# A gated linear unit over 8192 rows: four-row groups packed in place in three slots, instead of two input slots and two output slots

## The chip, the cores and the metric

The kernel runs on one core of a Trainium2 chip. The metric is the device time in microseconds of one execution of the whole program; lower is better. The profile is taken from an execution of its own, and its span (from the first to the last instruction that it records) is a little shorter than the device time.

## What is computed

The input `x` has 8192 x 8192 float32 values. Each row is cut into two halves, `a` (the first 4096 columns) and `b` (the last 4096), and the output has 8192 x 4096 values:

```python
def reference(x):
    a, b = np.split(x, 2, axis=-1)
    return a * (1 / (1 + np.exp(-b)))
```

That is one sigmoid and one multiplication for each output value. 268.4 MB are read and 134.2 MB written, with no value used twice.

## The kernel before

Two consecutive rows go to each of the 128 partitions, so a tile is 256 rows, 8 MB of input and 4 MB of output, and there are 32 tiles. Two slots hold input tiles (64 KB per partition each), two more hold output tiles (32 KB per partition each): 192 KB per partition in all.

```python
    R = 2
    SLOTS = 2
    n_tiles = n_rows // (P * R)
    x_t = x.rearrange("(n p r) m -> n p (r m)", p=P, r=R)
    out_t = out.rearrange("(n p r) m -> n p (r m)", p=P, r=R)
    xs = [pool.tile([P, R * n_cols], fp32, name=f"x_sb{k}") for k in range(SLOTS)]
    os = [pool.tile([P, R * half], fp32, name=f"o_sb{k}") for k in range(SLOTS)]
    ...
    for i in range(n_tiles):
        ...
        load = nc.sync.dma_start(out=xs[i % SLOTS], in_=x_t[i])
        ...
        if 0 < i < n_tiles - 1:
            parts = [(slice(0, R), slice(0, half))]
        else:
            w = half // 2
            parts = [
                (slice(r, r + 1), slice(c * w, (c + 1) * w)) for r in range(R) for c in range(2)
            ]
        ...
        for k, (r, c) in enumerate(parts):
            b = rows[:, r, 1, c]
            sig = nc.scalar.activation(out=b, in_=b, func=SIG)
            mul = nc.vector.tensor_mul(out=packed[:, r, c], in0=rows[:, r, 0, c], in1=b)
            ...
            if i == n_tiles - 1 and k > 0:
                store(chunks[k - 1])
        store(chunks[-1] if i == n_tiles - 1 else slice(0, R * half))
```

Loads are issued by SyncE (SP), stores by ScalarE (ACT), each on its own DMA queue. ACT computes the sigmoid of `b` in place, VectorE (DVE) multiplies into the output slot. A tile is one sigmoid and one multiplication of 8192 elements per partition (both rows); the first and the last tile are done in four pieces of 2048, and the last tile's output is stored piece by piece. A load into a slot waits for the multiplication that last read the slot; a multiplication or a sigmoid waits for the store that last read the output slot. Most of the other code in the loop (`implied`, `add_manual_dep`) names waits that follow from these and are dropped. `_launch_early` moves the first load ahead of the start-up barrier, and `_close_on_sync` shortens the end of the program; both stay as they are.

Of the kernel before, what the change touches and what calls it, by code (L numbers as in the profile page):

```python
# [1 line left out]

# [4 lines left out]


def _tiles(ctx, tc, x, out):

    nc = tc.nc
    P = nc.NUM_PARTITIONS  # L20
    DEP = mybir.DependencyInfo(mybir.DependencyClass.Sync, mybir.DependencyReason.DATA)
    fp32 = mybir.dt.float32
    SIG = mybir.ActivationFunctionType.Sigmoid

    n_rows, n_cols = x.shape
    half = n_cols // 2
    R = 2
    SLOTS = 2
    n_tiles = n_rows // (P * R)
    x_t = x.rearrange("(n p r) m -> n p (r m)", p=P, r=R)  # L30
    out_t = out.rearrange("(n p r) m -> n p (r m)", p=P, r=R)

    pool = ctx.enter_context(tc.tile_pool(name="io", bufs=1))
    xs = [pool.tile([P, R * n_cols], fp32, name=f"x_sb{k}") for k in range(SLOTS)]
    os = [pool.tile([P, R * half], fp32, name=f"o_sb{k}") for k in range(SLOTS)]

    def implied(later, *earlier):
        for e in earlier:
            tc.declare_no_dep(later.ins, e.ins, reason="follows from the waits that are kept")

    gone = [{k: [] for k in ("loads", "sigs", "muls", "stores")} for _ in range(SLOTS)]
    last_stores = [[] for _ in range(SLOTS)]
    for i in range(n_tiles):
        old = gone[i % SLOTS]
        freed = last_stores[i % SLOTS]
        now = {k: [] for k in old}
        rows = xs[i % SLOTS].rearrange("p (r h m) -> p r h m", r=R, h=2)
        packed = os[i % SLOTS].rearrange("p (r m) -> p r m", r=R)

        load = nc.sync.dma_start(out=xs[i % SLOTS], in_=x_t[i])  # L50
        implied(load, *old["loads"], *old["sigs"])
        now["loads"].append(load)

        if 0 < i < n_tiles - 1:
            parts = [(slice(0, R), slice(0, half))]
        else:
            w = half // 2
            parts = [
                (slice(r, r + 1), slice(c * w, (c + 1) * w)) for r in range(R) for c in range(2)
            ]  # L60
        def store(cols):
            ins = nc.scalar.dma_start(out=out_t[i, :, cols], in_=os[i % SLOTS][:, cols])  # L62
            now["stores"].append(ins)

        chunks = []
        for k, (r, c) in enumerate(parts):
            b = rows[:, r, 1, c]
            sig = nc.scalar.activation(out=b, in_=b, func=SIG)  # L68
            mul = nc.vector.tensor_mul(out=packed[:, r, c], in0=rows[:, r, 0, c], in1=b)  # L69
            implied(sig, *old["sigs"], *old["muls"], *old["loads"])  # L70
            implied(mul, *old["muls"], *old["loads"], *now["loads"])
            by_sigmoid = i % 2 == 1 and len(parts) == 1
            implied(mul, *(s for s in old["stores"] if by_sigmoid or s not in freed))
            if by_sigmoid:
                for s in freed:
                    tc.add_manual_dep(sig.ins, s.ins.name, DEP, reason="frees the output slot")
            tc.keep_in_program_order(sig)
            now["sigs"].append(sig)
            now["muls"].append(mul)
            chunks.append(slice(r.start * half + c.start, r.start * half + c.stop))  # L80
            if i == n_tiles - 1 and k > 0:
                store(chunks[k - 1])
        store(chunks[-1] if i == n_tiles - 1 else slice(0, R * half))
        for s in now["stores"]:
            implied(s, *old["loads"], *old["sigs"], *old["muls"], *now["loads"], *now["sigs"])
        for k in old:
            old[k] += now[k]
        last_stores[i % SLOTS] = now["stores"]


def _launch_early(nc):

    SP = mybir.EngineType.SP
    entry, body = (b.instructions for b in nc.main_func.blocks[:2])
    load = next(i for i in body if i.engine == SP and i.opcode == "DMACopy")
    assert not load.sync_info.on_wait
    body.remove(load)
    where = next(k for k, i in enumerate(entry) if i.engine == SP and i.opcode == "Drain")  # L100
    entry.insert(where, load)


def _close_on_sync(nc):

    SP, POOL = mybir.EngineType.SP, mybir.EngineType.Pool  # L110
    ACT = mybir.EngineType.Activation
    block = nc.main_func.blocks[2].instructions
    waits = block[0]
    assert waits.engine == SP and waits.opcode == "Drain" and len(waits.sync_info.on_wait) > 1
    pool = [i for i in block if i.engine == POOL]
    drain1, gather1, release1, reset, clear, drain2, gather2, release2 = pool
    assert reset.is_reset_sema and clear.opcode == "ISA"
    others = [i for i in block[1:] if i.engine != POOL]
    arrive = [i for i in others[: len(others) // 2] if i.opcode == "Drain"]
    assert len(arrive) == 4  # L120
    body = nc.main_func.blocks[1].instructions
    last = [i for i in body if i.engine == ACT and i.opcode == "DMACopy"][-1].sync_info.on_update[0].id
    final = [w for w in waits.sync_info.on_wait if w.id == last]
    assert len(final) == 1

    def event(engine, wait, update=()):
        return mybir.InstEventSemaphore(
            name=nc.get_next_instruction_name(),
            engine=engine,
            debug=waits.debug,  # L130
            sync_info=mybir.SyncInfo(on_wait=[wait], on_update=list(update)),
        )

    n = len(block)
    for lo, hi in ((reset.reset_range_start, last), (last + 1, reset.reset_range_stop)):
        if lo < hi:
            nc.gpsimd.sem_clear(range(lo, hi))
    clears = block[n:]
    assert clears and all(i.opcode == "ISA" for i in clears)
    back = mybir.SyncUpdate(  # L140
        sync_type="semaphore",
        id=last,
        ant_name=final[0].ant_name,
        update_mode="sem-sub-imm",
        update_value=final[0].wait_value,
        update_reg=None,
    )
    block[:] = [
        *arrive,
        drain1,  # L150
        gather1,
        *(event(POOL, w) for w in waits.sync_info.on_wait if w.id != last),
        reset,
        *clears,
        drain2,
        event(SP, final[0], [back]),
    ]


@with_exitstack  # L160
def kernel(
    ctx: ExitStack,
    tc: tile.TileContext,
    x: bass.AP,
    out: bass.AP,
):
    nc = tc.nc
    with ExitStack() as pools:
        _tiles(pools, tc, x, out)
    tc.close()  # L170
    tc.compile()
    _launch_early(nc)
    _close_on_sync(nc)


# [1 line left out]
_INS = ['x']  # L177
_OUTS = [((8192, 4096), 'float32')]


# [23 lines left out]
```

## Time and profile before

| What | Value |
|---|---|
| Device time, median of 3 (lowest, highest) | 933.31 us (933.03, 933.4) |
| Span of the profiled execution | 931.7 us |
| DVE busy | 278.7 us, 38 multiplications |
| ACT busy | 227.1 us, 38 sigmoids and a table load |
| Sigmoid and multiplication of 8192 elements | 7031 ns and 8692 ns |
| Sigmoid and multiplication of 2048 elements | 1903 ns and 2288 ns |
| SP's queue waiting for a multiplication | 859.9 us in total, 30 times |

How to read it: "busy" is the time in which an engine executes; the issuing of a DMA isn't counted. DMA queue q1 is SP's and carries the loads, q10 is ACT's and carries the stores. The share of a queue is the time that its packets took, as a share of 16 DMA engines over the span. "To landing" is the time from the issue of a DMA to its completion. A line number such as L69 is a line of the kernel.

### The profile page before, as it was taken

The numbers are of one execution on the slowest core, as the hardware profiler recorded it, in microseconds if no ns is written. First come the engines' busy times: TensorE is split into PE (matmuls) and PEld (weight loads), VectorE is DVE, ScalarE is ACT, GpSimd is POOL, SyncE is SP. The second block draws the span as 40 slices with busy tenths as digits, with TensorE's granted clock in tenths as the row PEclk, the third lists the DMA queues.
The fourth block names the chain that finished last, engine by engine and source line by source line (L and its number), as shares of the span: only waits on it lengthen the run. The fifth ranks groups of instructions, "written<-read, shape, count | busy, mean of one in ns | idle before, by whom it ended". The sixth has DMA issues, their size and how long they took to land.

```text
span 931.7 us, 247 instructions
## 1 busy us (share of the span) xinstructions
DVE 278.7 (30%) x38; ACT 227.1 (24%) x39; POOL 0.2 (0%) x4
## 2 busy tenths in 40 slices
DVE  0333213333133331233312333123331233312333
ACT  1323330233311333113331133311333113332033
POOL 0000000000000000000000000000000000000000
DMA  9999999999999999999999999999999999999999
GB/s 405 428 450 428 422 456 405 450 428 428 450 418 438 428 436 442 428 428 450 447 408 428 442 459 428 413 460 411 450 428 425 453 408 447 428 428 450 425 430 405
DMA packets 9649, 402.67 MB, mean 432 GB/s; under 512 B 1072, under 2 KB 1072, under 8 KB 1072
## 3 DMA queue, kind: packets, MB, share of 16 engines
q1 hardware_dynamic: 4608, 268.44, 66.6%
q10 hardware_dynamic: 5040, 134.22, 33.4%
q14 instruction: 1, 0.01, 0.0%
HBM read 268.44 MB, written 134.22 MB: 432 GB/s over the span
## 4 chain that ended last, share of the span: by engine, by line
DMA 73%; DVE 15%; ACT 12%; issue 0%; ACTq 0%
DMA x_sb<-in_x_dram 73%; DVE o_sb L69 15%; ACT x_sb L68 12%; ACTq L62 0%; ACTq L68 0%
## 5 line engine op out<-in xcount | busy, mean ns | idle before, releaser
L69 DVE TENSOR_TENSOR o_sb<-x_sb 128x8192 f32<-128x8192 f32 (+1 forms) x38 | 278.7, 7344 | 647.1 <-ACT x_sb L68 647.1
L68 ACT ACTIVATE x_sb<-x_sb 128x8192 f32<-128x8192 f32 (+1 forms) x38 | 225.8, 5952 | 695.6 <-DMA x_sb<-in_x_dram 694.4
L68 ACT ACT_TABLE_LOAD x1 | 1.3, 1283 | 0.8 <-PEq L188 0.8
L188 POOL MEMSET const-bfloat16-1.0<- 128x1 bf16 x1 | 0.1, 102 | 0.0
L188 POOL MEMSET const-uint8-127<- 128x1 uint8 x1 | 0.1, 102 | 0.0
L188 POOL MEMSET const-float32-0.0<- 128x1 f32 x1 | 0.1, 99 | 0.2 <-issue 0.2
L188 POOL MEMSET const-float32-1.0<- 128x1 f32 x1 | 0.1, 99 | 0.0
## 6 DMA issues: line engine op xcount, KB each, us to landing
out_dram<-o_sb ACTq DMA_DIRECT2D x31, 4096.0 KB, 34.7
out_dram<-o_sb ACTq DMA_DIRECT2D x4, 1024.0 KB, 5.6
x_sb<-in_x_dram SPq DMA_DIRECT2D x32, 42.2
```

The lines of the kernel that those rows point to most:

```text
L68: sig = nc.scalar.activation(out=b, in_=b, func=SIG)
L69: mul = nc.vector.tensor_mul(out=packed[:, r, c], in0=rows[:, r, 0, c], in1=b)
L188: nc = _bacc.Bacc("TRN2", target_bir_lowering=False, num_devices=1)
```

## The change

Rows are taken in groups of four per partition (512 rows, 16 groups). A group's input is loaded in two halves of two rows, 8 MB each. There are three slots of 64 KB per partition, 192 KB in all as before: two called `firsts`, used in turn for the first half of a group, and one called `second` for every second half. There are no output slots. The products are written in place: those of the first half over the beginning of the group's `firsts` slot, those of the second half over its end, so that after both halves the slot holds the four output rows, packed. One store of 8 MB then writes them, 64 KB from each partition, and for each partition both ends of the store are contiguous. The purpose is to have fewer and larger stores, and to use the memory of the output slots for a third load slot.

Every half is computed row by row: two sigmoids and two multiplications of 4096 elements, where before one of each covered both rows.

A load into `second` waits for the multiplications that read `second`. A load into a `firsts` slot waits for the store that reads the slot; both loads are issued by SP in the order second half, then the next-but-one first half.

In the last group, the first half is stored by itself (4 MB) and by SP, whose queue then holds the last load ahead of it; the second half is computed in four pieces of 2048 elements and stored by ACT piece by piece, 1 MB each.

The core of the diff (cut; the lines that only declared which waits follow from others are removed with the rest of the old loop):

```diff
-    SLOTS = 2
-    n_tiles = n_rows // (P * R)
-    x_t = x.rearrange("(n p r) m -> n p (r m)", p=P, r=R)
-    out_t = out.rearrange("(n p r) m -> n p (r m)", p=P, r=R)
+    n_groups = n_rows // (P * 2 * R)
+    x_t = x.rearrange("(n p h r) m -> n h p (r m)", p=P, h=2, r=R)
+    out_t = out.rearrange("(n p h r) m -> n p (h r m)", p=P, h=2, r=R)
...
-    xs = [pool.tile([P, R * n_cols], fp32, name=f"x_sb{k}") for k in range(SLOTS)]
-    os = [pool.tile([P, R * half], fp32, name=f"o_sb{k}") for k in range(SLOTS)]
+    firsts = [pool.tile([P, R * n_cols], fp32, name=f"first{k}") for k in range(2)]
+    second = pool.tile([P, R * n_cols], fp32, name="second")
...
+    def load(g, h):
+        nc.sync.dma_start(out=second if h else firsts[g % 2], in_=x_t[g, h])
+
+    def compute(g, h, pieces, each=None):
+        src = second if h else firsts[g % 2]
+        rows = src.rearrange("p (r k m) -> p r k m", r=R, k=2)
+        packed = firsts[g % 2].rearrange("p (h r m) -> p h r m", h=2, r=R)[:, h]
+        w = half // pieces
+        for r in range(R):
+            for c in range(pieces):
+                cols = slice(c * w, (c + 1) * w)
+                b = rows[:, r, 1, cols]
+                sig = nc.scalar.activation(out=b, in_=b, func=SIG)
+                tc.keep_in_program_order(sig)
+                nc.vector.tensor_mul(out=packed[:, r, cols], in0=rows[:, r, 0, cols], in1=b)
+                if each is not None:
+                    each((h * R + r) * half + c * w, w)
+
+    def store(engine, g, lo, n):
+        engine.dma_start(out=out_t[g, :, lo : lo + n], in_=firsts[g % 2][:, lo : lo + n])
+
+    load(0, 0)
+    load(0, 1)
+    load(1, 0)
+    for g in range(n_groups):
+        last = g == n_groups - 1
+        compute(g, 0, 1)
+        if last:
+            store(nc.sync, g, 0, R * half)
+            waiting = []
+
+            def each(lo, n):
+                if waiting:
+                    store(nc.scalar, g, *waiting.pop())
+                waiting.append((lo, n))
+
+            compute(g, 1, 2, each)
+            store(nc.scalar, g, *waiting.pop())
+        else:
+            compute(g, 1, 1)
+            store(nc.scalar, g, 0, 2 * R * half)
+            load(g + 1, 1)
+            if g + 2 < n_groups:
+                load(g + 2, 0)
```

More of the change, by code (lines that the diff above doesn't have):

```diff
@@ L20, in _tiles @@
     P = nc.NUM_PARTITIONS
-    DEP = mybir.DependencyInfo(mybir.DependencyClass.Sync, mybir.DependencyReason.DATA)
     fp32 = mybir.dt.float32
@@ L35, in _tiles @@
-    os = [pool.tile([P, R * half], fp32, name=f"o_sb{k}") for k in range(SLOTS)]
[L37 to L55, printed above, removed]
-        else:
[L57 to L88, printed above, removed]
```

## The prediction

> **What bounds the kernel now.** I read the page's DMA lines first, because the two compute engines are busy only 30% and 24% of the span, then the chain, then the times to landing, then the stretches.
>
> ```profile
> span 931.7 us, 247 instructions
> ...
> DMA  9999999999999999999999999999999999999999
> ...
> DMA packets 9649, 402.67 MB, mean 432 GB/s; under 512 B 1072, under 2 KB 1072, under 8 KB 1072
> ...
> q1 hardware_dynamic: 4608, 268.44, 66.6%
> q10 hardware_dynamic: 5040, 134.22, 33.4%
> ...
> DMA 73%; DVE 15%; ACT 12%; issue 0%; ACTq 0%
> ...
> out_dram<-o_sb ACTq DMA_DIRECT2D x31, 4096.0 KB, 34.7
> out_dram<-o_sb ACTq DMA_DIRECT2D x4, 1024.0 KB, 5.6
> x_sb<-in_x_dram SPq DMA_DIRECT2D x32, 42.2
> ```
>
> All 40 slices have full DMA engines, and the shares of the two queues (q1 is SP's loads, q10 ACT's stores) add up to 100%. The chain seems to say otherwise, with 27% on ACT and DVE. But that chain only follows one load to the next through a sigmoid and a multiply; while they run, the other slot's load and the stores keep the DMA engines fed. The stretches confirm it (columns: stretch, its length, three engines' busy time with instructions, clock, DMA share, GB/s):
>
> ```profile
> 0.00:22.00 22.00, 0.00 (x0) 1.33 (x2) 0.20 (x4) 1.00 1.02 429
> 22.00:42.00 20.00, 8.90 (x4) 7.26 (x4) 0.00 (x0) 1.00 0.95 393
> 42.00:100.00 58.00, 17.39 (x2) 14.06 (x2) 0.00 (x0) 1.00 1.00 434
> 100.00:900.00 800.00, 241.70 (x28) 196.87 (x28) 0.00 (x0) 1.00 1.00 434
> 900.00:932.00 32.00, 10.68 (x5) 7.54 (x4) 0.00 (x0) 1.00 0.95 410
> ```
>
> From 42 to 900 us the rate is 434 GB/s without a break. 402.67 MB at 434 GB/s take 927.8 us, so of the 931.7 us only about 4 lie in the start and the end. No reordering can win much more than that; a change can, however, open gaps.
>
> **Why there is no gap now** is in the landing times. A load is issued every 29 us (two tiles in the 58.0 us from one same-slot load to the next in the chain) and takes 42.2 us to land; a store is issued every 29 us and takes 34.7. Both take longer than the interval, so neither queue runs empty: when a new load is issued, the one ahead of it has 42.2 - 29.0 = 13.2 us left. Nothing that is late by less than 13 us shows.
>
> **What the Trainium skill says.** "DMA: Bandwidth & Descriptors", section "Where 436 GB/s comes from", puts the ceiling at 435.2 GB/s; the trace's 434 agrees, so the middle is at the wall. The same page, "Queues, rings and completion order", says that each DMA engine alternates between the queues that have work, packet by packet. The trace agrees: q1's time is 0.666 x 16 x 931.7 us over 4096 packets of 64 KB (4608 less 512 completion writes), 2.42 us each; q10's, less 512 packets of 8 KB at 0.31, is 1.21 us for each of 3968 packets of 32 KB. One for one, that shares the traffic 2:1, just what loads and stores need. "Issuing engines are not separate DMA queues" says that a second queue adds no bandwidth; the sum of 100% agrees. The same page, "Latency and other measured facts", reports that copies within HBM lose rate where the partitions' row pitch is a large power of two (207 GB/s at 512 KiB, 214 with a padded pitch). The new loads have a pitch of 128 KiB where they had 64; no run here shows its effect, and I allow it a small chance only.
>
> **The change part by part.**
>
> 1. *Bytes and packets.* The bytes stay. Stores become 64 KB packets: 15 x 128 of them replace 30 x 128 of 32 KB. By the times above, 3840 x 1.213 - 1920 x 2.418 = 15 us of engine time, over 16 engines about 1 us. The last group keeps 4 MB in one and 4 MB in four pieces. **-1 us.**
>
> 2. *Row by row.* Sigmoids of 8192 elements take 7031 ns and of 2048, 1903; multiplies 8692 and 2288. By straight line, 4096 elements cost an estimated 3.61 and 4.42 us. A half is ready 3.6 + 2 x 4.42 = 12.5 us after its sigmoid starts, instead of 15.7. It costs an issue more per half on engines that idle 70% of the time: nothing. With 0.41 us from landing to sigmoid (before: landing 914.30, sigmoid 914.71) and 0.1 for the issue, 13.0 us pass from the landing of a second half to the next issues.
>
> 3. *Start.* Three loads, 24 packets deep on each engine, are queued from about 1.9 us; they last until 60 us. The second half of group 0 lands at 40.6, so the first store leaves at 53.6. No gap; the first store comes later, which saves nothing as the wall is bytes.
>
> 4. *End.* The first half's store stands in SP's queue behind the last load: 4 MB, 9.7 us of work, while the last half is computed. Pieces come after 0.4 + 1.9 + 2.3 = 4.6 us and then every 2.3 us, four of them up to 11.5 us, each 2.4 us of traffic. Work at hand until the last piece is 9.7 + 3 x 2.4 = 17 us: no gap. Before, tile 30's store (issued 901.7) filled the same stretch as well. **0 us.**
>
> 5. *The cycle of one group*, the step on which the answer turns. A group moves 16 load packets and 8 store packets per engine, 24 x 2.418 = 58.0 us. Let both issues be at 0: the 8 MB store, and the load into `second`; the load of the next first half is still in flight with X packets. The store's packets now weigh as much as the load's. Its first one starts some 4 to 6 us late: for the only store of before that met an empty queue, issued at 32.8, this shows:
>
> ```profile
> q1 hardware_dynamic: 32, 2.10, 85.1%
> q10 hardware_dynamic: 16, 0.52, 18.1%
> ```
>
> Those are the DMA packets from 32.8 to 39.5 us: two load packets per engine, then the first store packet, which the same view up to 38.8 does not have yet. So 6 us from issue to first packet; and the two load packets fill 0.851 x 16 x 6.7 / 32 = 2.85 us each instead of 2.42, a stall of about 0.9 us in all. Then 8 rounds of store and load, 8 x 4.84 = 38.7 us. With a typical 5 us ahead of them the store lands at 43.7 (44.7 with the stall). **Only then** may the load of group g+2's first half go, since its slot is the store's source. Its data flow 2.0 to 2.6 us after the issue (the first load of before: 21.9 to landing less 8 x 2.418), thus at about F = 46. But when is the queue empty? The second half's load lands at L, and the next issues are at L + 13.0. Without a gap the period is 58.0, so L = 45.0. That is before F: slack has shrunk from 13.2 us to about -1. A later L lets less of the next load run, half is given back: L = (45.0 + F)/2 = 45.5, and the period grows by **0.5 us**. With the 0.9 us stall in every group, F = 47 and L = (45.0 + 0.9 + 47)/2 = 46.5: **1.4 us**. With a quick first packet (3.7 us) F = 44.8: **0**. Fourteen groups wait so: 0, 7 or 20 us.
>
> *Sum:* 933.3 - 1.0 + 14 x 0.5 = 939.3; I take 940.0.
>
> **The rivals.** (a) *All hidden:* the store starts sooner, or a load issued just in time slips behind the running one: 932 us. For it: the needed slack is a single microsecond and the numbers are single observations. (b) *A stall at each restart of the store queue:* 933.3 - 1.0 + 20 = 952 us. For it: the stall was there the one time that an empty store queue was refilled; against it: that was the queue's first use. (c) *The memory dislikes 128 KiB pitch:* 1% of the loads' 620 us (0.666 x 931.7) would be 6 us, beside the others; visible as longer load packets. (d) *A compute engine binds:* 66 multiplies cost about 62 x 4.42 + 4 x 2.29 = 283 us of DVE; it cannot. (e) *Faster by the shorter latency:* the latency was hidden already, and the wall leaves 4 us.
>
> **Range and chances.** (a) gets 30%, the middle case 40%, (b) and beyond 30%. Two per cent is 18.7 us: faster needs 914.6, under the 925.2 us that the bytes take at 435.2 GB/s, as good as excluded. Slower needs over 952.0, where (b) has its centre: 15%. Range 931.5 to 955.
>
> **What would show it.** DMA share under 1.00 in the middle stretch, some 0.99 for 940 (434 becomes about 430 GB/s); 8192 KB stores landing after about 44 us; loads of `second` landing 45 to 46 us after issue; SP's queue waiting mostly for the store. Sigmoids and multiplies of 4096 at 3.6 and 4.4 us. Step 5 is wrong if the stores land after under 42 us or over 47, or if the middle stretch stays at 434; then 932 would be the time. A load packet that lasts longer than 2.42 us would mean (c). If store packets were split to 32 KB, the store would get a third of the traffic and land after some 60 us, and the time would go far above the range.

## The result and the profile after

The changed kernel takes 968.02 us (median of 4 runs, 964.2 to 968.68) against 933.36 us: 1.036 times the time, with a 95% interval of 1.034 to 1.038. The prediction, 940 us with a range up to 955, was too low by 28 us.

The page of the changed kernel, the lines that answer to those shown of before:

```profile
span 967.3 us, 310 instructions
...
DMA packets 7490, 402.67 MB, mean 416 GB/s; under 512 B 832, under 2 KB 832, under 8 KB 832
...
q1 hardware_dynamic: 4752, 272.63, 67.8%
q10 hardware_dynamic: 2736, 130.02, 31.1%
...
out_dram<-first SPq DMA_DIRECT2D x1, 4096.0 KB, 31.6
out_dram<-first ACTq DMA_DIRECT2D x4, 1024.0 KB, 8.1
first<-in_x_dram SPq DMA_DIRECT2D x16, 30.1
second<-in_x_dram SPq DMA_DIRECT2D x16, 47.4
out_dram<-first ACTq DMA_DIRECT2D x15, 44.4
```

The two queue lines hold the whole loss, in two parts. First, the shares add up to 98.9% instead of 100: in 1.1% of 967.3 us, 10.6 us, an average engine had no packet. Second, the load packets are longer. q1's time is 0.678 x 16 x 967.3 = 10493 us; less the 128 packets of SP's one store (1.213 us each) and over 4096 load packets that is 2.524 us each, where it was 2.42. With 256 load packets per engine, this makes 27 us. Together they cover the 36 us by which the span grew and the 1 us that the fewer store packets save.

The middle stretch, to compare with 434 GB/s at a share of 1.00 before:

```profile
100.00:900.00 800.00, 236.58 (x54) 192.30 (x54) 0.00 (x0) 1.00 0.99 415
```

The DMA share is the 0.99 that the prediction named, but the rate is 415 GB/s and not 430: a longer packet counts as busy time, so the share doesn't show it.

The waits of SP's queue (engine and line, what it waited for, total us, times, longest) show which transfer holds the loads back:

```profile
SPq L27 <- DMA out_dram<-first: 620.8, 14, 48.6
SPq L27 <- DVE first L40: 186.4, 15, 12.5
SPq L27 <- DMA second<-in_x_dram: 81.4, 14, 39.5
```

Fourteen loads waited for the 8 MB store. In the chain of waits (start, length, what) one group looks like this:

```profile
53.58 46.86 DMA second<-in_x_dram
100.48 0.05 issue
100.53 3.62 ACT second L38
104.18 8.77 DVE first L40 x2
112.97 46.96 DMA second<-in_x_dram
```

From 53.58 to 112.97 are 59.4 us for a group, where the packets need 58.0. Other groups take up to 62.8; the eleven from 53.58 to 718.56 us average 60.45. The packet records, read one by one, say where in a group the time goes. Per group and averaged over the engines, about 1.3 us are load packets that last longer just after the store is issued, 0.5 us are load packets that last longer elsewhere, mostly around the landing of the second half, and 0.65 us are idle. The idle time is uneven: about 5.2 of its 9 us lie in the one group that begins at 718.6 us.

The first of these terms can be read in the DMA view of the changed kernel from 112.9 to 118.6 us, right after the second store's issue:

```profile
q1 hardware_dynamic: 28, 1.84, 98.2%
q10 hardware_dynamic: 4, 0.26, 10.6%
```

28 load packets took 0.982 x 16 x 5.7 us, 3.20 us each instead of 2.42. (Shares of so short a window can add up to more than 100%, as a packet that begins in it counts in full.) It is the kind of stall that the kernel before showed once, with 0.9 us at its first store, and it now comes back at every 8 MB store but one, the one issued at 842.6 us.

### The profile page after: what moved, and what is told of

Its sections match the earlier page's. It is cut to its first block, busy times and chain, and to the rows that moved or that the text cites. A ratio compares the mean times of both kernels' runs of the same rounds, so it can differ in the third digit from the quotient of the medians.

```text
span 967.3 us, 310 instructions
## 1 busy us (share of the span) xinstructions
DVE 282.0 (29%) x66; ACT 229.6 (24%) x67; POOL 0.2 (0%) x4
## 4 chain that ended last, share of the span: by engine, by line
DMA 77%; DVE 13%; ACT 6%; another core or an unknown queue 3%; issue 0%; ACTq 0%; SPq 0%
DMA second<-in_x_dram 68%; DVE first L40 13%; ACT second L38 6%; DMA out_dram<-first 5%; DMA first<-in_x_dram 3%; ACT first L38 1%; ACTq L45 0%; ACTq L38 0%; SPq L27 0%
## 5 line engine op out<-in xcount | busy, mean ns | idle before, releaser
L40 DVE TENSOR_TENSOR first<-second 128x4096 f32<-128x4096 f32 (+1 forms) x34 | 140.4, 4171 | 381.4 <-ACT second L38 381.4
L40 DVE TENSOR_TENSOR first<-first 128x4096 f32<-128x4096 f32 x32 | 141.6, 4425 | 295.6 <-ACT first L38 293.9
L38 ACT ACTIVATE second<-second 128x4096 f32<-128x4096 f32 (+1 forms) x34 | 114.4, 3408 | 413.5 <-DMA second<-in_x_dram 412.2
L38 ACT ACTIVATE first<-first 128x4096 f32<-128x4096 f32 x32 | 114.0, 3608 | 312.8 <-DMA first<-in_x_dram 312.8
## 6 DMA issues: line engine op xcount, KB each, us to landing
second<-in_x_dram SPq DMA_DIRECT2D x16, 47.4
out_dram<-first ACTq DMA_DIRECT2D x15, 44.4
```

Of the source, the lines that this page charges most:

```text
L40: nc.vector.tensor_mul(out=packed[:, r, cols], in0=rows[:, r, 0, cols], in1=b)
```

## The experiments

Each run is one edit of the changed kernel, or of a run named with it, unless it says otherwise. "Load packets left" below means the load packets per engine that are issued and not yet finished when a store is issued, without the load that is issued in the same moment, counted in the packet records.

**A store per half.** The first half of a group is stored as soon as it is computed.

```diff
         compute(g, 0, 1)
+        store(nc.sync if last else nc.scalar, g, 0, R * half)
         if last:
-            store(nc.sync, g, 0, R * half)
 ...
-            store(nc.scalar, g, 0, 2 * R * half)
+            store(nc.scalar, g, R * half, R * half)
```

> Undoes one part: instead of one 8 MB store per group, each half is stored by itself (4 MB, 32 KB packets) as soon as it is computed; slots, loads, row-by-row work and the tail stay. Theory (the gap comes from the single late store: the store queue runs empty and restarts with a stall of 1.3 us each time, and the first slot comes free at 44 us of a cycle of 58): the second store lands after some 34 us, the wait for the slot has 10 us to spare, and the store queue is never empty, so 931 to 935 us, restart stall seen once only. Rival (the load's pitch of 128 KiB, the in-place writes or the row-by-row work cost the time): these all stay, so about 968 us.

Measured: 934.24 us, 1.0007 of before (0.9999 to 1.0016). The page's queues:

```profile
q1 hardware_dynamic: 4752, 272.63, 67.7%
q10 hardware_dynamic: 4896, 130.03, 32.3%
...
out_dram<-first ACTq DMA_DIRECT2D x30, 4096.0 KB, 40.1
```

The sum is 100% again, and a store lands 40.1 us after its issue while one is issued every 29, so the queue never runs empty. Just after an issue (the DMA view from 116 to 126 us) load packets are at 0.725 x 16 x 10 / 48 = 2.42 us:

```profile
q1 hardware_dynamic: 48, 3.15, 72.5%
q10 hardware_dynamic: 34, 1.05, 24.3%
```

The whole loss goes with the single late store. The in-place packing, the 128 KiB pitch, the three slots and the row-by-row work, which all stay, cost nothing that this run can show. The first slot's wait, though, did not end at 34 us as expected: the second store queues behind the first half's, and the slot is free some 40 us after the load of `second` is issued, only 4 us sooner than in the changed kernel.

**The same at half the size.** One row per half, 32 groups, second halves in pieces (`R = 1`, `compute(g, 1, 2)`).

> The same structure at half the size: one row per half, groups of two rows, slots of 32 KB, 32 groups instead of 16, the second half always in pieces of 2048. If the loss is paid per group in fixed times (restart stall, restart of the load after the store's landing, spread of the engines), 30 groups lose some 3.5 us each: about 1040 us. If it is paid per byte (pitch, larger packets), the time stays at about 968 us or falls, since the pitch is 64 KiB here.

Measured: 1029.34 us. Over 933 that is 96 us, some 3.2 for each of 30 groups with half the bytes: paid per group, not per byte.

**Half the size with six slots.** As the run before, with four slots for first halves and two for second ones (cut; three more loads are issued ahead of the loop).

```diff
-    R = 2
+    R = 1
+    F, S = 4, 2
 ...
-            load(g + 1, 1)
-            if g + 2 < n_groups:
-                load(g + 2, 0)
+            if g + S < n_groups:
+                load(g + S, 1)
+            if g + F < n_groups:
+                load(g + F, 0)
```

> As the run with two-row groups, but with four first slots and two second slots of 32 KB, in the same 192 KB: nothing is changed but how long a load has to wait for its slot. Theory (the wait for the slot): all of the loss is gone but for the restart stall of the store queue, if that recurs: 932 to 937 us when it is hidden, up to 30 x 1.3 = 39 us more when each restart costs. Rival (packets, pitch): like the two-row groups with three slots.

Measured: 972.54 us, the median of four runs from 964.98 to 984.77; without the slowest 1.037 of before (1.0331 to 1.041). That is at the far end of what was expected. The stretches show two halves of a run:

```profile
100.00:500.00 400.00, 120.36 (x40) 96.87 (x40) 0.00 (x0) 1.00 1.00 430
560.00:940.00 380.00, 107.28 (x37) 87.90 (x36) 0.00 (x0) 1.00 0.98 405
940.00:972.00 32.00, 13.41 (x5) 10.92 (x5) 0.00 (x0) 1.00 0.69 294
```

Up to 500 us the restarts after the first cost little: with 8 or more load packets (32 KB here) left, packets grew by 0.0 to 0.2 us per store. From 550 us on, with 6 to 7.4 left, by 0.9 to 1.3 us. In between, the 16 engines had drifted apart: their completions of one load were spread over 0.5 to 4 us until 250 us, but over some 20 to 31 us from 500 us nearly to the end, with most engines close together and one or two far behind. So 7 packets left is a mean over unequal engines. At the end most engines are through long before the last, hence the 0.69. More slots alone are no cure, and why the engines drift isn't settled by these runs.

**Both rows of the second half at once.** One sigmoid and one multiplication of 8192 elements.

```diff
+        if pieces == 0:
+            b = rows[:, :, 1, :]
+            sig = nc.scalar.activation(out=b, in_=b, func=SIG)
+            tc.keep_in_program_order(sig)
+            nc.vector.tensor_mul(out=packed, in0=rows[:, :, 0, :], in1=b)
+            return
 ...
-            compute(g, 1, 1)
+            compute(g, 1, 0)
```

> Undoes one part: the second half of each group but the last is computed by one sigmoid and one multiplication of 8192 elements, so the time from its landing to the next issues grows from 13.0 to 16.3 us. Theory: this time is part of the cycle's critical chain, and half of any change in it is given back, as the period is (landing of the second half + this time), with L = (58.0 - this time + F)/2: 1.65 us more per group, 14 to 15 groups, 968 + 24 = 992 us. Rival (compute latency is hidden, the queue alone sets the time): 968 us. If nothing is given back: 968 + 15 x 3.3 = 1017 us.

Measured: 1052.4 us, over 6 us per group for 3.3 us of latency. All three expectations miss, even the largest. Groups alternate: the store lands after 43 us in one and after 52 to 54 in the next. The DMA view of a quick group (133 to 168 us), then of a slow one (195 to 230 us):

```profile
q1 hardware_dynamic: 128, 7.34, 48.4%
q10 hardware_dynamic: 112, 7.34, 48.4%
```

```profile
q1 hardware_dynamic: 97, 6.29, 51.5%
q10 hardware_dynamic: 94, 6.16, 44.6%
```

By size there are 112 and 96 load packets: 0.484 x 560 / 112 = 2.42 us each, and 0.515 x 560 / 96 = 3.00 us through the whole transfer (560 is 16 engines times 35 us). The slow groups have some 6 us of idle time besides. In the quick groups 3.0 load packets were left at the store's issue, in the slow ones 2.0 or 2.1, in every group of the run. Longer compute thus cost far beyond its own length. It leaves fewer load packets for the store to meet, and the slow transfers go with the fewest; the changed kernel's worst group, the one at 718.6 us, also has the fewest of its run, 2.2. That the number causes them is not shown: other groups of that run with 2.3 or 2.4 left had no slow transfer and at most 1.3 us of idle time.

**Shorter pieces.** The opposite: `compute(g, 1, 2)` for every second half.

> The changed kernel with every second half computed in four pieces of 2048, so 11.6 instead of 13.0 us pass from landing to the next issues. By the rule of the halves 0.7 us less per group, 968 - 10 = 958 us; the run with both rows at once showed that longer compute costs far more than half where under 3 load packets are left at the store's issue, so shorter compute should also end the slow transfers: 950 to 958 us. Rival (compute is hidden): 968 us.

Measured: 951.87 us, 1.0205 of before (1.0172 to 1.0238): 16 us less for 14 times 1.6 us of latency (11.0 us pass from landing to issue instead of 12.5), well over a half. Load packets left: 3.1 to 4.1. Four of the 14 later restarts of the store queue lengthened no packets by more than 0.1 us, and the mean is 0.7 us, where the changed kernel has 1.3. Yet the four had 3.2 to 3.6 load packets left, and a restart with 4.1 left cost 1.2 us: within this range the number left doesn't decide by itself.

**One store, but in packets of 32 KB,** and loads contiguous over the partitions. Rows are mapped differently, so the store has two runs of 32 KB per partition.

```diff
-    x_t = x.rearrange("(n p h r) m -> n h p (r m)", p=P, h=2, r=R)
-    out_t = out.rearrange("(n p h r) m -> n p (h r m)", p=P, h=2, r=R)
+    x_t = x.rearrange("(n h p r) m -> n h p (r m)", p=P, h=2, r=R)
+    out_t = out.rearrange("(n h p r) m -> n p h (r m)", p=P, h=2, r=R)
```

> The single store of 8 MB per group stays, but rows are mapped so that it consists of two pieces of 32 KB per partition, and each load is contiguous over all partitions (pitch 64 KiB as in the kernel before). Theory (queues alternate packet by packet): the store's packets weigh half as much, it lands after 45 to 63 us instead of 44, the first slot comes free later and the loads starve: about 9 us more per group than the ideal, 1030 to 1070 us. Rival (the 128 KiB pitch or the 64 KB store packets cost the time): under 968 us, towards 933.

Measured: 983.85 us.

```profile
out_dram<-first ACTq DMA_DIRECT2D x15, 8192.0 KB, 52.6
```

The direction is right: smaller packets make the store land later, after 52.6 us instead of 44.4. The size is not: a group takes about 61.5 us, 3.5 more than its packets need and not 9. The loads of `second` land after 49.0 us, so the store has the engines to itself for the last 3.6, which the estimate left out. The pitch changes together with the packets here; that 64 KiB doesn't save the kernel speaks against the pitch, and the store-per-half kernel, at full rate with 128 KiB, rules it out.

This run also bounds what the load packets left can explain. Its later stores restart beside 5 to 7 of them, and each of these restarts still lengthens load packets by 0.8 to 1.0 us. The DMA view from 418 to 424 us, right after the store's issue at 417.98:

```profile
q1 hardware_dynamic: 31, 2.03, 94.5%
q10 hardware_dynamic: 10, 0.33, 12.6%
```

31 load packets took 0.945 x 16 x 6 us, 2.93 us each instead of 2.42.

**The restart by itself.** A plain kernel with one row per partition, separate output slots, and a store for every second tile only. Half of the output is left out, so that the store queue runs empty before each store. With two input slots:

> Measures the restart stall by itself. Tiles of one row per partition, two input slots of 32 KB, two output slots; only every second tile is stored, so half of the output is left out and the store queue runs empty before each of 32 stores; no load ever waits for a store. Packets alone: 64 x 8 x 1.213 + 32 x 8 x 0.611 = 777.5 us, about 781 with start and end. At each store's issue some 2 to 3 load packets per engine are left. Theory (an empty store queue that restarts beside a nearly empty load queue costs some 1.1 us): 781 + 31 x 1.1 = 815 us, load packets lengthened in the first 4 us after each store. Rival (the stall in the changed kernel comes from the wait for the slot): 781 us.

and with five:

> As the run with two input slots, half of the output left out again, but with five input slots, so some 26 load packets per engine wait at each store's issue. If a restart of the store queue always costs its stall: 815 us as with two slots. If it costs only where little load work is queued (as the run with six slots suggests, where the stall came when under 8 packets were left): 781 us.

Measured: 802.82 and 789.8 us. Both expectations left out the last tile's tail, about 8 us. The difference, 13 us, is what the packet records show as lengthened packets: 0.4 us per store with some 2 load packets left (0.0 to 1.0), 0.0 with 26. After the first store, an empty store queue was thus free beside 26 load packets of 32 KB. Beside 2 it cost, here less than expected.

**The restart in the kernel's own structure.** Only one half of each group is stored (all but the last group's), the other half's output is left out. First variant: the first half's rows (`store(nc.scalar, g, 0, R * half)`).

> The changed kernel, but each group's store (all but the last group's) carries only the first half's rows, 4 MB in 32 KB packets at the same moment; the second half's output is left out. The store now lands some 34 us after its issue, so the first slot is free 10 us before the second half lands: the late slot is gone, the restart of an empty store queue beside about 3 load packets stays. Packets alone: 32 x 8 x 2.418 + 16 x 8 x 1.213 + 32 x 0.309 = 784 us, 788 with start and end. If the restart stall of about 1.2 us is a cost of its own: 788 + 14 x 1.2 = 805 us. If the stall comes only with the late slot: 788 us.

Measured: 789.44 us. The store didn't leave at the planned moment: it depends on the first half alone and was issued before the second half's sigmoids, with 11 load packets left. Second variant: the second half's rows (`store(nc.scalar, g, R * half, R * half)`).

> The restart stall with few loads behind it, without the late slot. As the run that stores first halves only, but each group's store (all but the last's) carries the second half's rows and so leaves only when the second half is computed, as in the changed kernel; the first half's output is left out. In the run with first halves the store left earlier than planned, with 11 load packets per engine queued, and no restart but the first showed a stall. Here about 2.6 are queued. The store lands some 34 us after its issue, 10 us before the second half: no late slot. If the restart stall depends on the load work queued: 788 + 14 x 1.3 = 806 us, with load packets lengthened right after each store's issue. If it needs the late slot: 789 us as in that run.

Measured: 813.4 us. The two variants have the same packets and bytes and differ in the moment of the store. Their stretches from 60 to 740 us, first variant, then second:

```profile
60.00:740.00 680.00, 246.56 (x56) 199.42 (x56) 0.00 (x0) 1.00 1.00 434
```

```profile
60.00:740.00 680.00, 237.78 (x54) 192.31 (x54) 0.00 (x0) 1.00 0.99 420
```

In the first no store but the very first lengthens a packet. In the second the fourteen later restarts cost 13.8 us with 2 to 4 load packets left, though one of them, with 3.0 left, cost nothing. Most of the remaining 10 us are at the end of each load of `second`: with fewer bytes this landed after 37 us, not 45, so the late slot that this run was to be without was still there, with 2 us to spare. The two terms are told apart by their place in the packet records, not by a run that has one without the other.

**A late slot beside a busy store queue.** The store-per-half kernel, with the load of the next first half held back until the second half ahead of it has landed.

```diff
 ...
-            load(g + 1, 1)
+            ahead = load(g + 1, 1)
             if g + 2 < n_groups:
-                load(g + 2, 0)
+                late = load(g + 2, 0)
+                tc.add_manual_dep(late.ins, ahead.ins.name, DEP, reason="a late slot")
```

> The kernel with a store per half, but the load of the next first half is held back until the second half ahead of it has landed, so the load queue is empty for about 2.2 us in each of 14 groups: the late slot of the changed kernel, without its empty store queue. Theory (only a moment in which both queues are short of work costs): stores fill the 2.2 us, so 934 to 937 us. Rival (a load queue that runs empty costs by itself): 14 x 1 to 2.2 us more, 948 to 965 us.

Measured: 941.3 us, 1.0077 of before (1.0063 to 1.0091), between the two. Where the load queue runs dry (the DMA view from 220.5 to 226.5 us), the stores take over:

```profile
q10 hardware_dynamic: 79, 2.10, 81.0%
q1 hardware_dynamic: 16, 0.98, 39.2%
```

By size 64 store packets in 0.81 x 96 us are 1.21 us each, the plain time, and there is no idle time. But the stores so brought forward leave their queue empty when the next one comes, with 4.1 to 5.1 load packets left, and these restarts stall by 0.1 to 0.7 us, 6 us in all. That is where most of the 7 us are. A dry load queue cost nothing in this run while stores were queued; it cost through the restart that it led to.

**The end alone.** The store-per-half kernel with the last group's first half stored by ACT.

> The kernel with a store per half, with the last group's first half stored through ACT's queue like all others, instead of through SP's behind the last load: the change's treatment of the end, undone alone. The end is bound by bytes in either case (the engines have 17 us of work until the last piece is there): within 1.5 us of the 934.2 us of the store-per-half kernel.

Measured: 934.25 us, 1.0004 of before (0.9996 to 1.0012). The first half stored behind the last load neither gains nor costs.

No version beat the kernel before; the store-per-half kernel and it are equal within the interval.

## Why the prediction was wrong

- Step 1, packets: right. 64 KB store packets take 2.42 us, and the packets' plain time falls by 1.1 us.
- Step 2, row by row: right in the sizes of the work. 4096 elements take 3608 ns and 4425 ns (estimated 3.61 and 4.42 us). The 0.41 us from landing to sigmoid was a misreading: in the chain of before, the load issued at 872.68 us lands 42.01 us later, at 914.69, and the sigmoid starts at 914.71. So 12.5 us pass from landing to issue, not 13.0, which by the prediction's own sum would have made step 5 milder.

```profile
872.68 42.01 DMA x_sb<-in_x_dram
914.69 0.02 issue
914.71 1.92 ACT x_sb L68
```

- Step 3, start: the first store was issued at 53.6 us as worked out, with some luck: the second half landed at 41.1 us instead of 40.6, and the half microsecond of step 2 made up for it.
- Step 4, end: right, by the run of the end alone.
- Step 5, the cycle: the place was right, the sum was not, and this is the step that failed. The store landed after 44.4 us (predicted: 43.7 without a stall, 44.7 with), SP waited mostly for it, and the slack was indeed gone. But `second` landed after 47.4 us, where I had 45.5 or 46.5, and the group grew by 2.4 us, where I had 0.5, or 1.4 with the stall.
- Within step 5, three terms were mis-sized. *The stall at each restart of the store queue* had 30% in the prediction, with the excuse that it was the queue's first use. It came back with 13 of the 14 later 8 MB stores, at 1.4 us on average instead of 0.9; once it stayed away. *The handover at the second half's landing* was counted as idle time alone; load packets also lengthen there, which makes most of 0.5 us per group. *The spread of the engines* was left out: the 16 completions of one load are spread over 0.6 to 1.0 us in the kernel before and over up to 8.1 us, mostly 2 to 5, after, and every wait is for the last engine. What the spread costs by itself no run shows.
- The rule that half of a delay is given back failed as well: the pieces gained 1.15 us per group for 1.6 us, both rows at once lost 6 for 3.3. The rule took the restart's cost as fixed; over the runs it varied from nothing to 1.7 us, and with both rows at once whole transfers were slow.
- The signs by which step 5 was to be told wrong did not show its failure. It was to be wrong if the stores landed after under 42 or over 47 us, and they landed after 44.4. Longer load packets were to mean (c), and they came without it, with the restarts and the handovers.
- Rival (a), all hidden, is refuted. Rival (b) named the largest term and was still too small, at 952 us. Rival (c), the pitch, is refuted: the store-per-half kernel runs at 434 GB/s with it. The run with 32 KB packets is slow without it. (d) and (e) did not come about, as predicted. The remark that 32 KB packets would land after 60 us and put the time far above the range was half right: 52.6 us and 984.

What stays open is why a restarting store queue lengthens the load packets ahead of it, and what decides whether it does. Beside 11 load packets of 64 KB it did not, after the first store; beside 2 to 7 it mostly did, but six of the 42 later restarts in the changed kernel, the run with pieces and the run with second halves only cost 0.1 us or less, all with 3.0 to 3.6 left. The runs show that the single late store costs the 36 us, not the mechanism of the stall.

## What to carry to other kernels

In this kernel, which is bound by DMA, the time was kept where no queue ran empty while the other was short of work. So compare each transfer's time to landing with the interval at which it is issued: a landing shorter than the interval means a queue that restarts. Merging two stores into one larger one saved 1 us of packets here and took away the overlap that kept the queue filled, for 36 us. A stall seen once in a trace deserves the question of how often the change will repeat its conditions.

## What the runs showed of the hardware that was not expected

- A store queue that restarted beside 2 to 4 load packets of 64 KB per engine lengthened those packets by 0.7 to 1.3 us on average (the 14 later restarts of three runs each); beside 5 to 7, in the run with 32 KB store packets, by 0.8 to 1.0 us; beside 11, by 0.0 us. The first store of a run stalled in every run examined, by 0.4 to 1.4 us, even beside 27 packets of 32 KB.
- With both rows at once, in the groups with only 2.0 or 2.1 load packets left, packets of both queues stayed slow for a whole transfer: load packets at 3.00 us instead of 2.42.
- The DMA engines of one core drifted apart in the run with six slots: the 16 completions of one load came to lie up to 31 us apart, while in the kernel before they stay within 1.0 us throughout.
